# Filler transposes before the first rows of x, and the second sequence's blocks turned in pairs

## The chip, the cores and the metric

The kernel runs on one core of a Trainium2 chip. Four compute engines work side by side, each through its own list of instructions in the order in which the program was built: TensorE (PE; its weight loads are shown apart as PEld), VectorE (DVE), ScalarE (ACT) and GpSimd (POOL). SyncE (SP) computes nothing here and issues DMA transfers. An instruction starts when its engine has reached it and what it waits for is there; one that waits holds up all that stands behind it on its engine. The metric is the device time of one execution in microseconds.

## What is computed

The reference is one encoder layer over two sequences of 512 rows with 1024 features each. It normalizes the rows, projects them, runs a state-space branch (S5, both directions) and an attention branch with a window, merges the two by gates, and ends in a squared-ReLU MLP. For this change only the beginning matters:

```python
def rms_norm(x, g):
    xf = x.astype(jnp.float32)
    y = xf * lax.rsqrt(jnp.mean(xf * xf, axis=-1, keepdims=True) + EPS)
    return (y * g.astype(jnp.float32)).astype(x.dtype)
```

The normalized rows are multiplied with wide weights, among them the 8 blocks of 128 columns that feed the state-space branch ("u"), and 8 blocks each for its two gates. The state-space branch also needs tables: powers of discretized eigenvalues, worked out from a small parameter array (lam) and from coefs.

## The kernel before

**Rows of x.** The 1024 rows are eight tiles of 128 rows (xt; tiles 0 to 3 are the first sequence, 4 to 7 the second), loaded one after the other by SyncE ahead of the weights. square_rows (L287) lets ScalarE square a tile and sum each row (L290), and GpSimd turn the sum into a scale (L292, L293). scale_rows (L295) lets VectorE multiply the tile by it (L296).

**Turning.** turn_rows(s, k) (L298 to L305) takes the k-th block of 128 columns from the four tiles of sequence s, turns each with a transpose on TensorE against the identity (ident, written once at the start by GpSimd) into one PSUM buffer (sps for even k, tps for odd k, two buffers each), and then makes the two halves of a split number: ScalarE writes the high half times the gain (L303), VectorE the remainder, the low half (L304). The traces name these two outputs act.

**Columns.** A column of weights (c_raw, fetched in two halves by SyncE, in fetch, L153) is split the same way: split (L167) lets ScalarE write c_hi (L175) and VectorE c_lo (L176), and after the second half calls for the next c_raw. products (L180) is a generator that issues one matmul at each step, three for each k (high by high, high by low, low by high, 24 in all to a column and sequence), with 128x512 results in one of three PSUM buffers named acc. The generator splits the next column's two halves behind its steps 3 and 9. pull(units) (L260) takes steps from this list, two units a matmul, so pull(6) issues the three matmuls of one k and pull(12) six. some(n) (L388) issues the next n instructions of the tables' arithmetic, small VectorE instructions on 128x64.

**The order of the start.** From L270 on the written order is the order on all five engines. For the first sequence (L399) a loop over k = 0 to 7 turns block k, squares or scales a tile of the second sequence in between, and from k = 2 pulls the three matmuls of an earlier k, so the matmuls stay two blocks behind. Then, for the second sequence:

```python
scale_rows(7)
pull(12)
for k in range(KT):
    turn_rows(1, k)
    pull(6)
    some(4)
```

After this loop come four GpSimd instructions, a small matmul, `while some(4): pull(6)`, and copies of the tables (br_p L429 and L430, ei and er L433 to L435). Behind them the section ends, and from there only TensorE and GpSimd keep the written order; on the others a scheduler places the instructions of tables() (L464 and on) by its own estimates of when they can start, and may lift them into the stretch above. It does so with the load of coefs for the first group (bcx, L469, on SyncE's queue) and with the two copies cw (L480, L481) that read it on VectorE.

Of the kernel before, what the change touches and what calls it, by code (L numbers as in the profile page):

```python
# [19 lines left out]
P = 128  # L20
# [4 lines left out]
KT = D // P  # L25
# [38 lines left out]
def hybrid_layer(ctx, tc, x, rel, onehot, w_qkv, w_ug, vectors, lam, coefs, w_glu, w_out, ln2,  # L64
                 w_up, w_down, out):
    nc = tc.nc
    V, S, PE, GP, SP = nc.vector, nc.scalar, nc.tensor, nc.gpsimd, nc.sync
# [12 lines left out]
    def acc():  # L80
        return ps_acc.tile([P, 512], F32, tag="acc", name="acc")

    def tps():
        return ps_t.tile([P, 512], F32, tag="tps", name="tps")

    def sps():
        return ps_s.tile([P, 512], F32, tag="sps", name="sps")
# [16 lines left out]
    ident = const.tile([P, P], F32, name="ident")  # L104
# [155 lines left out]
    def pull(units):  # L260
        while units > 0:
            cost = next(filler, None)
            if cost is None:
                return
            units -= cost
            phase["units"] -= cost
# [4 lines left out]
    with tc.tile_pool(name="xin", bufs=1, reuse_waits="tile") as xin, tc.tile_pool(name="ssmc", bufs=1) as sc:  # L271
# [23 lines left out]
        def scale_rows(t):  # L295
            V.tensor_scalar_mul(xs[t], xs[t], scales[t])  # L296

        def turn_rows(s, k):  # L298
            ps = tps() if k % 2 else sps()
            for i in range(4):  # L300
                PE.transpose(ps[:, i * P:(i + 1) * P], xs[s * 4 + i][:, k * P:(k + 1) * P], ident)
            h = hT[s][0][:, k, :]
            S.activation(h, ps, AF.Copy, scale=gain_1[:, k:k + 1])  # L303
            V.scalar_tensor_tensor(hT[s][1][:, k, :], ps, gain_1[:, k:k + 1], h.bitcast(F32),  # L304
                                   op0=ALU.mult, op1=ALU.subtract)  # L305
# [82 lines left out]
        def some(n):  # L388
            return len(list(itertools.islice(coefs_left, n)))
# [9 lines left out]
        for k in range(KT):  # L399
            turn_rows(0, k)  # L400
            if k % 2 == 0:
                square_rows(4 + k // 2)
            elif k > 1:
                scale_rows(3 + k // 2)
            if k in (4, 5):
                split(k - 4)
            if k > 1:
                pull(6)
        scale_rows(7)
        pull(12)  # L410
        for k in range(KT):
            turn_rows(1, k)
            pull(6)
            some(4)
        GP.tensor_scalar_mul(gain_q, gain_q, HD ** -0.5)
        GP.tensor_scalar_mul(nsink, nsink, -1.0)
        GP.tensor_tensor(dmask, ident[:, 0:CH], ident[:, 32:32 + CH], op=ALU.add)
# [762 lines left out]
    with tc.tile_pool(name="glu", bufs=1, reuse_waits="tile") as gpool, \  # L1180
# [10 lines left out]
        for u in range(2, 2 * KT):  # L1191
            m, s = divmod(u, 2)
# [436 lines left out]
```

## Time and profile before

| | before |
|---|---|
| median of 3 runs (fastest, slowest) | 1474.6 us (1472.87, 1474.95) |
| profiled execution, its own time | 1474.11 us |
| span of its profile | 1472.3 us |
| TensorE busy, instructions | 1442.3 us (98% of the span), 8074 |
| weight loads busy | 1230.4 us (84%) |
| VectorE busy, instructions | 1101.7 us (75%), 1989 |
| ScalarE busy, instructions | 760.0 us (52%), 1362 |
| GpSimd busy, instructions | 210.4 us (14%), 372 |
| HBM read, written | 173.22 MB, 90.21 MB |

How to read it: the profile comes from one execution. A row of the timeline has the start and the duration in microseconds, the engine, the line, the operation, what it writes and reads with partitions by elements and types, how many instructions of one kind follow each other, and in brackets the idle time of the engine just before and what ended it. Matmuls are pipelined, so their rows overlap and a matmul's row is longer than the distance to the next. A chain row has start, length, engine and line of one piece of the work that ended last, followed back from the end. A row for stretches has the start and end of a stretch, its length, each engine's busy time with its instructions, TensorE's granted clock (1.00 is full), the share of time in which the DMA engines were busy, and what they moved in GB/s. Shares of busy time are means over stages with different limits.

### The profile page before, as it was taken

The page shows a single profiled execution, that of the slowest core. Times are in us where ns is not written, and L with a number is a line of the kernel's source. Part 1 is how long each engine was busy: PE and PEld are TensorE (multiplying, and loading weights), DVE is VectorE, ACT ScalarE, POOL GpSimd, SP SyncE. Part 2 cuts the span into 40 slices and gives each one's busy share as a digit, 9 for nine tenths or more (in the row PEclk, how much of TensorE's full clock was granted, in tenths as well). Part 3 has the DMA queues.
Part 4 walks back from the last instruction along what each step waited for, and adds up shares of the span by engine and source line. Part 5 has one row for each costly group of instructions (what it writes and reads, how often), then busy time and mean ns, then how long its engine had stood idle before and what let it go on. Part 6 is the DMA issues. An engine that isn't in the chain of part 4 may idle for free.

```text
span 1472.3 us, 22141 instructions
## 1 busy us (share of the span) xinstructions
PE 1442.3 (98%) x8074; PEld 1230.4 (84%) x8074; DVE 1101.7 (75%) x1989; ACT 760.0 (52%) x1362; POOL 210.4 (14%) x372
## 2 busy tenths in 40 slices
PE   6999999999999999999999999999999999999998
PEld 4788888879899999998888878888888888888787
DVE  7998859986645899997984588777776597475553
ACT  6677762225535888776343355544544444333332
POOL 3133351002322444222100000000000000000000
PEclk9999999999999999999999999999999999999999
DMA  4455459328940445367553244444443893454441
GB/s 177 142 172 172 165 167 362 116 100 299 346 163 16 144 151 158 107 234 232 191 193 114 86 157 175 148 153 145 146 150 115 326 338 108 158 184 146 127 129 58
DMA packets 102877, 249.16 MB, mean 169 GB/s; under 512 B 12234, under 2 KB 23754, under 8 KB 102768
## 3 DMA queue, kind: packets, MB, share of 16 engines
q1 hardware_dynamic: 60240, 139.55, 29.2%
q0 software_dynamic: 16896, 53.53, 10.5%
q10 hardware_dynamic: 25632, 54.67, 9.9%
q8 instruction: 64, 1.05, 0.3%
q14 instruction: 45, 0.37, 0.1%
HBM read 173.22 MB, written 90.21 MB: 179 GB/s over the span
## 4 chain that ended last, share of the span: by engine, by line
PE 82%; DVE 7%; ACT 4%; DMA 3%; issue 3%; POOL 1%; ACTq 0%; SPq 0%; DVEq 0%; POOLq 0%
PE acc L185 14%; PE bank L117 14%; PE bank L118 13%; PE bank L116 13%; PE acc L813 5%; PE acc L123 3%; PE acc L117 2%; PE acc L118 2%; PE acc L116 2%; PE po L896 2%; PE sps L864 2%; PE sps L547 2%; PE tps L880 2%; PE acc L835 1%; PE sps L645 1%
## 5 line engine op out<-in xcount | busy, mean ns | idle before, releaser
L185 PE MATMUL acc<-act,c_hi 128*128 128x512 f32 x768 | 250.5, 401 | 1.0 <-DVE act L304 0.9
L117 PE MATMUL bank<-b_lo,a_hi 128*128 128x512 f32 x448 | 174.6, 390 | 1.4 <-DVE b_lo L1498 1.4
L118 PE MATMUL bank<-b_hi,a_lo 128*128 128x512 f32 x448 | 174.3, 389 | 0.0
L116 PE MATMUL bank<-b_hi,a_hi 128*128 128x512 f32 x448 | 173.5, 389 | 0.0
L185 PEld LDWEIGHTS acc<-act,c_hi 128*128 128x128 f32 x768 | 142.6, 190 | 29.2 <-DVE act L304 2.4
L185 PE MATMUL acc<-act,c_lo 128*128 128x512 f32 x384 | 153.2, 399 | 0.0
L1497 ACT CAST a_hi<-d_a 128x1024 fp32r<-128x1024 f32 x56 | 59.0, 1054 | 179.3 <-PE bank L117 177.7
L116 PE MATMUL bank<-act,act 128*128 128x512 f32 x368 | 143.3, 389 | 0.5 <-ACT f_sum L1322 0.5
L117 PE MATMUL bank<-act,act 128*128 128x512 f32 x368 | 143.3, 389 | 0.2 <-DVE act L1281 0.2
L118 PE MATMUL bank<-act,act 128*128 128x512 f32 x368 | 143.2, 389 | 0.0
L1498 DVE TENSOR_TENSOR a_lo<-d_a,a_hi 128x1024 fp32r<-128x1024 f32 x56 | 68.5, 1224 | 99.7 <-ACT a_hi L1497 99.7
L813 PE MATMUL acc<-w_hi,act 128*128 128x256 f32 x512 | 114.2, 291 | 0.0
L117 PEld LDWEIGHTS bank<-b_lo,a_hi 128*128 128x128 f32 x448 | 84.1, 188 | 19.6 <-DVE b_lo L1498 2.4
L116 PEld LDWEIGHTS bank<-b_hi,a_hi 128*128 128x128 f32 x448 | 84.1, 188 | 17.6
L118 PEld LDWEIGHTS bank<-b_hi,a_lo 128*128 128x128 f32 x448 | 84.1, 188 | 17.4
L813 PEld LDWEIGHTS acc<-w_hi,act 128*128 128x128 f32 x512 | 87.1, 190 | 3.7
L185 PEld LDWEIGHTS acc<-act,c_lo 128*128 128x128 f32 x384 | 72.8, 190 | 14.0 <-DVE c_lo L176 0.5
L116 PEld LDWEIGHTS bank<-act,act 128*128 128x128 f32 x368 | 69.1, 188 | 15.3 <-ACT f_sum L1322 0.9
L117 PEld LDWEIGHTS bank<-act,act 128*128 128x128 f32 x368 | 69.1, 188 | 14.9 <-DVE act L1281 0.5
L874 ACT ACTIVATE p<-p,nmx 128x257 f32<-128x257 f32 (+1 forms) x128 | 72.1, 564 | 17.9 <-DVE nmx L868 16.7
L118 PEld LDWEIGHTS bank<-act,act 128*128 128x128 f32 x368 | 69.1, 188 | 14.2
L123 PE MATMUL acc<-act,gc_hi 128*128 128x512 f32 x256 | 80.8, 394 | 0.0
(332 smaller groups left out, 3422.1 us busy)
## 6 DMA issues: line engine op xcount, KB each, us to landing
d_a<-a_scr SPq DMA_DIRECT2D x56, 512.0 KB, 3.6
raws<-in_w_up_dram SPq DMA_DIRECT2D x32, 512.0 KB, 4.1
a_scr<-t ACTq DMA_DIRECT2D x64, 256.0 KB, 2.9
k<-in_w_down_dram SPq DMA_DIRECT2D x32, 512.0 KB, 6.1
c_raw<-in_w_ug_dram SPq DMA_DIRECT2D x48, 256.0 KB, 3.7
ct_scr<-ctab POOLq DMA_DIRECT2D x16, 576.0 KB, 3.7
ctab_in<-ct_scr POOLq DMA_DIRECT2D x16, 576.0 KB, 7.4
y_scr<-y_scr POOLq DMA_DIRECT2D x16, 512.0 KB, 5.5
```

Of the source, the lines that this page charges most:

```text
L116: PE.matmul(ps, a[0], b[0], start=first, stop=False)
L117: PE.matmul(ps, a[0], b[1], start=False, stop=False)
L118: PE.matmul(ps, a[1], b[0], start=False, stop=last)
L123: PE.matmul(ps, w[wi][:, k, :], rows[yi], start=k + p == 0, stop=k == KT - 1 and p == 2)
L185: PE.matmul(ps, w[wi][:, k, :], hT[s][hi][:, k, :], start=n == 0, stop=n == 3 * KT - 1)
L547: PE.matmul(ps[:, i * P:(i + 1) * P], bm[:, ri, g, :], u_sb[:, gp * SH + g, :], start=True, stop=True)
L813: PE.matmul(self.ps, hT[sq][act][:, k, col:col + P], w[:, k % 4, :], start=i == 0, stop=i == 3 * KT - 1)
L864: PE.matmul(ps[:, 0:self.nk], qs, kk[:, self.k0 * P:self.k1 * P], start=i == 0, stop=i == 1)
L874: S.activation(p, p, AF.Exp, bias=self.nmx[:, h:h + 1], scale=-1.0, accum_out=self.sums[:, h, self.qb:self.qb + 1])
L880: PE.transpose(pt[:, h * P:(h + 1) * P], self.p[:, h, 1 + i * P:1 + (i + 1) * P], ident)
L1497: S.copy(hi, src)
L1498: V.tensor_sub(lo, src, hi.bitcast(F32))
```

## The change

It has two parts. In turn_rows, the first call (s = 0, k = 0) now issues transposes of the identity into an acc buffer that nothing reads: 32 before the first transpose of x and 8 before each of the three others (busy, L300 to L302 in the changed file). And the loop over the second sequence takes two blocks a turn, with pull(12) and some(8) behind the two, so four transposes and four more stand together, then six matmuls.

```diff
+        idle = acc()
+
+        def busy(n):
+            for i in range(n):
+                PE.transpose(idle[:, i % 4 * P:(i % 4 + 1) * P], ident, ident)
+
         def turn_rows(s, k):
             ps = tps() if k % 2 else sps()
             for i in range(4):
+                if s + k == 0:
+                    busy(8 if i else 32)
                 PE.transpose(ps[:, i * P:(i + 1) * P], xs[s * 4 + i][:, k * P:(k + 1) * P], ident)
...
-        for k in range(KT):
+        for k in range(0, KT, 2):
             turn_rows(1, k)
-            pull(6)
-            some(4)
+            turn_rows(1, k + 1)
+            pull(12)
+            some(8)
```

Lines of the changed file stand 8 or 9 further down: L301, L303 and L304 become L309, L311 and L312, and L429, L469, L480 and L481 become L438, L478, L489 and L490. idle is taken once and takes one of the three acc buffers at the start.

On TensorE the program begins, before, with the blocks of x (xt):

```order
L301 MATMUL sps<-ident,xt 128x128 x4
L301 MATMUL tps<-ident,xt 128x128 x4
L301 MATMUL sps<-ident,xt 128x128 x4
L185 MATMUL acc<-act_103,c_hi 128x512
L185 MATMUL acc<-act_104,c_hi 128x512
```

and after the change with the filler transposes (L302):

```order
L302 MATMUL acc<-ident 128x128 x32
L309 MATMUL sps<-ident,xt 128x128
L302 MATMUL acc<-ident 128x128 x8
L309 MATMUL sps<-ident,xt 128x128
L302 MATMUL acc<-ident 128x128 x8
L309 MATMUL sps<-ident,xt 128x128
L302 MATMUL acc<-ident 128x128 x8
L309 MATMUL sps<-ident,xt 128x128
L309 MATMUL tps<-ident,xt 128x128 x4
```

The four blocks of the first set now stand apart, each behind its filler transposes; from the second set on the order of TensorE is as before until the second sequence's loop.

On VectorE, in the stretch of the first sequence's first blocks, the rows before are these (act_104 is the low half of the first sequence, cw the copies that read bcx):

```order
L176 TENSOR_TENSOR c_lo<-c_raw,c_hi 128x512 x2
L304 SCALAR_TENSOR_TENSOR act_104<-sps,vec,act_103 128x512
L304 SCALAR_TENSOR_TENSOR act_104<-tps,vec,act_103 128x512
L304 SCALAR_TENSOR_TENSOR act_104<-sps,vec,act_103 128x512
L480 TENSOR_TENSOR cw<-bcx 128x128
L481 TENSOR_TENSOR cw<-bcx 128x128
L304 SCALAR_TENSOR_TENSOR act_104<-tps,vec,act_103 128x512
```

and after the change:

```order
L176 TENSOR_TENSOR c_lo<-c_raw,c_hi 128x512 x2
L489 TENSOR_TENSOR cw<-bcx 128x128
L312 SCALAR_TENSOR_TENSOR act_104<-sps,vec,act_103 128x512
L490 TENSOR_TENSOR cw<-bcx 128x128
L312 SCALAR_TENSOR_TENSOR act_104<-tps,vec,act_103 128x512
L312 SCALAR_TENSOR_TENSOR act_104<-sps,vec,act_103 128x512
L312 SCALAR_TENSOR_TENSOR act_104<-tps,vec,act_103 128x512
```

The first copy cw moved ahead of the first low half, the second one behind it; both stood behind the third low half. The diff has no line on this: it is where the scheduler puts them in the changed program.

On ScalarE, behind the second sequence's loop, the rows before are these (c_hi is the high half of a column's weights, up a finished column):

```order
L175 CAST c_hi<-c_raw 128x512
L198 COPY up<-acc 128x8x64
L429 COPY br_p<-pr 64x8x64
L430 COPY br_p<-pr 64x8x64
L207 DMA u_scr<-up 128x1024
L433 COPY ei<-pi 64x512
L434 COPY ei<-pi 64x512
```

and after the change:

```order
L175 CAST c_hi<-c_raw 128x512
L198 COPY up<-acc 128x8x64
L175 CAST c_hi<-c_raw 128x512
L207 DMA u_scr<-up 128x1024
L438 COPY br_p<-pr 64x8x64
L439 COPY br_p<-pr 64x8x64
L442 COPY ei<-pi 64x512
```

The second high half of the next column, which stood behind all copies of ei and er, now stands ahead of br_p, and so does, on VectorE, its low half, behind which the next c_raw is fetched. On SyncE's queue four loads of c_raw now stand between the first load of bcx and the first load of u_sb (a finished column read back), where three stood; the order on GpSimd is as before.

## The prediction

> **What bounds the kernel now.** I read the page's head and chain first, then the chain of the first 62 us in order of time, and then the stretches that the change touches.
>
> ```profile
> span 1472.3 us, 22141 instructions
> PE 82%; DVE 7%; ACT 4%; DMA 3%; issue 3%; POOL 1%; ACTq 0%; SPq 0%; DVEq 0%; POOLq 0%
> ...
> 25.66 1.42 DVE xt L296 x2
> 27.12 0.34 PE sps L301
> ...
> 28.21 0.75 DVE act L304
> ...
> 43.36 0.44 DVE pr L371
> 43.81 0.34 ACT br_p L429
> ...
> 51.37 3.39 DMA c_raw<-in_w_ug_dram
> ```
>
> Over the whole span TensorE is the bound (82% of the chain), but the change lies in the first 60 us, where the chain hops: x must land, TensorE turns its blocks, ScalarE squares the rows of the second sequence, at 25.66 VectorE scales the last of them, TensorE turns them at 27.12, and from 28.21 to 43.8 VectorE's instructions carry it, then ScalarE's and a load of c_raw. Whatever is lost or won ahead of 25.66 is handed on down this list. The next view is busy time by stretch.
>
> ```profile
> core 0: us, PE busy (x) PEld busy (x) DVE busy (x) ACT busy (x) POOL busy (x), PEclk, DMA share, GB/s
> 0.00:12.00 12.00, 1.43 (x3) 0.55 (x3) 5.40 (x21) 7.17 (x12) 6.38 (x18) 1.00 0.86 309
> ...
> 19.00:25.00 6.00, 5.02 (x28) 3.65 (x27) 4.70 (x8) 5.54 (x10) 1.24 (x4) 1.00 0.12 44
> 25.00:44.00 19.00, 18.71 (x94) 14.30 (x95) 17.12 (x56) 8.84 (x16) 2.89 (x7) 1.00 0.05 17
> 44.00:60.00 16.00, 14.91 (x69) 11.63 (x68) 15.31 (x37) 13.06 (x34) 0.31 (x1) 1.00 0.47 148
> 326.20:329.60 3.40, 1.59 (x12) 1.28 (x11) 0.22 (x1) 2.36 (x3) 0.00 (x0) 1.00 0.39 154
> 329.70:333.00 3.30, 3.30 (x13) 2.82 (x12) 0.46 (x1) 2.75 (x5) 0.00 (x0) 0.50 0.00 0
> ```
>
> TensorE stands still for 10.6 of the first 12 us; ScalarE fills 5.54 of the 6.00 us after 19; TensorE idles 0.29 us between 25 and 44 and 1.09 us between 44 and 60. The last two rows show the clock: a stretch with 1.59 of 3.40 us busy is followed by one at a granted 0.50.
>
> **TensorE's clock at the start.** The clock column reads 1.00 before 19 us, but the durations say otherwise.
>
> ```profile
> 7.78 0.48 PE L301 MATMUL sps<-ident,xt 128*128 128x128 f32 x1 [7.78 <-DVE xt L296]
> 9.30 0.48 PE L301 MATMUL sps<-ident,xt 128*128 128x128 f32 x1 [1.05 <-DVE xt L296]
> 11.38 0.48 PE L301 MATMUL sps<-ident,xt 128*128 128x128 f32 x1 [1.60 <-DVE xt L296]
> 12.96 0.47 PE L301 MATMUL sps<-ident,xt 128*128 128x128 f32 x1 [1.10 <-DVE xt L296]
> 13.22 1.06 PE L301 MATMUL tps<-ident,xt 128*128 128x128 f32 x4
> 14.08 1.06 PE L301 MATMUL sps<-ident,xt 128*128 128x128 f32 x4
> 18.14 0.63 PE L185 MATMUL acc<-act,c_lo 128*128 128x512 f32 x1
> ...
> 30.02 0.39 PE L185 MATMUL acc<-act,c_lo 128*128 128x512 f32 x1
> 31.39 0.60 PE L301 MATMUL sps<-ident,xt 128*128 128x128 f32 x4
> ```
>
> The same matmul takes 0.63 us at 18 and 0.39 at 30, four transposes 1.06 and 0.60: the start runs at half clock. Four cold transposes follow each other in 14.08 - 13.22 = 0.86 us, 0.215 each. The first set's four blocks come one by one, as rows of x are scaled: at 7.78, 9.30, 11.38 and 12.96.
>
> **Part one, the filler transposes.** They need ident alone.
>
> ```profile
> 1.03 0.28 POOL masks.py:199 TENSOR_SCALAR_AFFINE_SELECT ident<-ident 128x128 f32<-128x128 f32 x1
> ```
>
> So they start near 1.4 us. 32 x 0.215 = 6.9 us cold, to 8.3; the first rows of x are ready at 7.78. If this busy stretch lifts the clock on the way, as the one from 12.96 to 19 did before, the first group ends before 8, each group of 8 takes about 8 x 0.11 = 0.9 us (half of 0.215 each) inside the 1.5 to 2.1 us between two blocks of x, and the real transposes at 12.96 run in half the time. Then they add nothing, and the whole stretch 13 to 19 could be faster. What that is worth is decided by who is late next, and here the row order of VectorE speaks: the first read of bcx (cw) now stands ahead of the first low half (L304) instead of behind the third.
>
> ```profile
> 8.36 0.33 SPq L469 DMA_DIRECT2D bcx<-in_coefs_dram  x1
> bcx<-in_coefs_dram SPq DMA_DIRECT2D x1, 256.0 KB, 8.4
> ...
> 14.62 0.74 DVE L304 SCALAR_TENSOR_TENSOR act<-sps,vec,act 128x512 fp32r<-128x512 f32 x1
> ...
> 15.41 0.29 PEld L185 LDWEIGHTS acc<-act,c_hi 128*128 128x128 f32 x1 [0.36 <-DVE act L304]
> 15.81 0.75 DVE L304 SCALAR_TENSOR_TENSOR act<-tps,vec,act 128x512 fp32r<-128x512 f32 x1 [0.45 <-ACT act L303]
> 16.47 0.74 DVE L304 SCALAR_TENSOR_TENSOR act<-sps,vec,act 128x512 fp32r<-128x512 f32 x1
> 17.13 0.28 DVE L480 TENSOR_TENSOR cw<-bcx 128x128 f32<-128x128 f32 x1
> 17.33 0.28 DVE L481 TENSOR_TENSOR cw<-bcx 128x128 f32<-128x128 f32 x1
> 17.52 0.69 ACT L303 ACTIVATE act<-tps,vec 128x512 fp32r<-128x512 f32 x1
> ...
> 19.42 0.69 ACT L303 ACTIVATE act<-sps,vec 128x512 fp32r<-128x512 f32 x1 [1.21 <-PE sps L301]
> ```
>
> The bcx transfer is issued at 8.36 and lands 8.4 us later, at 16.76, behind the eight loads of x on the same queue; nothing in the change moves it. Before, cw came at 17.13 and waited for nothing. Now VectorE, which was ready for the first low half at 14.62, stands at cw until 16.78; 0.20 later (17.33 - 17.13) the first low half starts, at 16.98, and ends at 17.73 instead of 15.36: 2.4 us late. Queued behind it are all the other low halves, the scaling of rows 4 to 7 and the next c_lo; and on TensorE the second matmul of the first three waits for it (the 15.41 row), with the transposes of k = 3, 4, 5 behind that, for which ScalarE's L303 waits.
>
> What follows from 17.73, at the two clocks:
> - Full clock: second matmul 0.23, then as from 30.02 (third matmul) to 31.39 + 0.60 = 31.99, the end of the second next four transposes: 1.97. So 17.73 + 0.03 + 2.20 = 19.96, and L303 of k = 4 starts at 19.98 against 19.42: **+0.56 us**. (The second low half, 16.98 + 0.66 + 0.20 = 17.84 to 18.59, is in time.)
> - Half clock throughout: before, the same chain took 19.42 - (14.62 + 0.74) = 4.06 us. 17.73 + 4.06 = 21.79: **+2.4 us**.
>
> From L303 of k = 4 on ScalarE is nearly full, so this shift reaches 27.1 and, over VectorE's full stretch, everything behind it. Which clock? TensorE has nothing to do from about 14.3 (12.96, plus 0.24 for the warm last block, 8 x 0.11 for two more sets and 0.23 for one matmul) to 17.76, some 3.4 us. A shorter gap cost the clock later on:
>
> ```profile
> 328.93 0.71 PE L645 MATMUL sps<-st,ctab_in 128*128 128x128 f32 x4 [1.81 <-ACT st L615]
> ```
>
> After this 1.81 us gap the clock was at 0.50 for 3.3 us. I expect the same in or just behind the new gap, for part of the chain, and take the middle: **+1.5 us**, bounds +0.56 and +2.4. [...]
>
> **Part two, blocks in pairs.** Instruction counts stay: 32 transposes, 48 matmuls, 8 of L303 and L304, 32 of some(). On TensorE four transposes go ahead of three matmuls, and the columns in this loop read the first sequence, so they wait for none of it. TensorE idles only 0.29 us from 25 to 44, so at most 0.3 can be gained; VectorE is the bound and its list is only permuted, 0.66 us a low half with L303 coming at a similar pace: 0, bounds -0.3 and +0.3.
>
> The new order reaches one stage further: the second half of the next c_hi and c_lo goes ahead of the br_p copies.
>
> ```profile
> 49.06 0.62 ACT L175 CAST c_hi<-c_raw 128x512 fp32r<-128x512 f32 x1
> ...
> 50.66 0.69 DVE L176 TENSOR_TENSOR c_lo<-c_raw,c_hi 128x512 fp32r<-128x512 f32 x1
> ...
> 54.78 0.62 ACT L175 CAST c_hi<-c_raw 128x512 fp32r<-128x512 f32 x1 [1.82 <-DMA c_raw<-in_w_ug_dram]
> ...
> 56.79 0.87 PE L534 MATMUL tps<-ident,bpre 128*128 128x128 f32 x6 [0.34 <-DVE bpre L511]
> ```
>
> The c_hi of 49.06 moves ahead of the br_p copy of 43.81, its c_lo with it, so the c_raw load of 51.37 is issued some 6 us sooner and ScalarE's 1.82 us wait can go; SP's u_sb load goes behind one more c_raw, by 0.33 us of issue. TensorE can win at most the 1.09 us it idles from 44 to 60. Against that, 0.62 us of ScalarE and 0.69 of VectorE are put in front of the chain to the first transposes of the tables, for which TensorE waits at 56.79 (VectorE's bpre): up to 0.6 us lost. The two sides overlap; I take 0, bounds -1.1 and +0.6.
>
> **Sum.** The profiled execution took 1474.11 us, 1.8 more than its span and 0.5 under the median of 1474.6. 1474.11 + 1.5 + 0 + 0 = **1475.6 us**.
>
> **Rivals.**
> 1. *The clock gain comes through.* If bcx is in by 14.7, or VectorE's wait is covered, the transposes of k = 4 end before 18 at full clock, and ScalarE's 1.21 us of waiting before L303 of k = 4 goes, and some 0.2 more with an earlier k = 3 (17.52 row): k = 4 starts near 18.0, -1.4 us, 1472.7; with the whole of the -1.1 it is 1471.6. For: everything but bcx is there. Against: DMA is busy 0.86 of the first 12 us, and the landing would have to be 2 us sooner.
> 2. *The clock stays at half until after 24 us* (slower). If transposes do not lift it, the filler takes 6.9 us, each group of 8 another 1.7, and the first set ends at 8.3 + 3 x 1.72 + 4 x 0.215 + 0.25 = 14.6 instead of 12.96 + 0.47 = 13.43; bcx still hides that, but TensorE is cold at 17.76: +2.4. A cold k takes 3 x 0.43 + 0.86 = 2.15 us; ScalarE asks for k = 6 about 1.1 us after k = 5, so a clock not full by 24 us adds 1.05: +3.5, 1477.6. It decides from a wake-up later than 24. For: the busy stretch from 12.96, which began with transposes, was lifted only at 19. Against: the stretch from 329.7 was lifted within 3.3 us, so from 17.76 the clock should be back at about 21 to 23. [...] The trace cannot settle it: no stretch of transposes alone stands in it.
> 3. *The shift is given back* in the 1.09 us of idle between 44 and 60: within 0.5 of before, 1474.1.
>
> **Chances.** Forecast 0.60; rival 1, 0.14; rival 2, 0.15; rival 3, 0.11. A difference under 0.2% (2.95 us) is about what a measurement can tell from none. Half of the first rival (with the whole of part two's gain and a lucky run: the shown runs span 2.1 us) reaches past -0.2%, and most of the second, with a few of the forecast's upper end, past +0.2%: faster 0.07, same 0.79, slower 0.14. Range: from rival 1 with part two's gain, 1471.6, to rival 2 with part two's loss, 1477.6 + 0.6 = 1478.2, each end a fourth of the run spread further out: 1471.1 to 1478.7.
>
> **What would show it.** VectorE's cw starting at about 16.8 behind an idle of some 2 us laid to the bcx load, the first L304 ending near 17.7; TensorE idle near 14.3 to 17.8; L303 of k = 4 near 20 (full clock) or 21 to 22 (half); filler transposes of 0.11 us spacing at some point before 8 if they lift the clock, 0.215 to the end if not; c_raw issued near 45. I am wrong if cw does not wait, if the first low half ends before 16, or if the stages from 60 on stand more than 3 us from where they stood.

## The result

| | before | changed kernel |
|---|---|---|
| median of 12 runs | 1474.41 us | 1477.16 us |
| ratio to before, 95% interval | 1 | 1.0023, 1.0014 to 1.0032 |
| profiled execution, its own time | 1474.11 us | 1475.65 us |
| span of its profile | 1472.3 us | 1473.9 us |
| TensorE busy, instructions | 1442.3 us, 8074 | 1448.0 us, 8130 |
| VectorE busy | 1101.7 us | 1101.3 us |

The changed kernel is slower by 0.23%; between the two profiled executions it is 1.54 us, and the forecast was +1.5 us. One of the 12 runs of the changed kernel, 2421 us long at a mean granted clock of 0.556, is left out of the ratio, and the median of its other 11 runs is 1476.62 us, 2.21 above before.

First the chain that ended last, in order of time, of the changed kernel: start, length, engine and line of each piece.

```profile
1.64 6.51 DMA xt<-in_x_dram
8.17 8.39 DMA bcx<-in_coefs_dram
16.79 0.76 DVE act L312
17.59 0.75 PE acc L185 x2
18.34 0.85 PE tps L309 x4
...
27.60 1.42 DVE xt L296 x2
29.07 0.34 PE sps L309
...
46.16 0.43 DVE pr L379
46.62 1.19 ACT br_p L438
```

The load of bcx is now on the chain: it follows the load of x and ends at 16.56, and the first low half (L312) follows it. The scaling of the last two tiles (L296) starts at 27.60, where it was 25.66 before: **1.94 us late**. br_p comes at 46.62 instead of 43.81, 2.81 late.

Next VectorE's timeline around the first low half, and under it TensorE's and ScalarE's in the same stretch.

```profile
13.25 1.29 DVE L176 TENSOR_TENSOR c_lo<-c_raw,c_hi 128x512 fp32r<-128x512 f32 x2
16.58 0.29 DVE L489 TENSOR_TENSOR cw<-bcx 128x128 f32<-128x128 f32 x1 [2.04 <-DMA bcx<-in_coefs_dram]
16.79 0.74 DVE L312 SCALAR_TENSOR_TENSOR act<-sps,vec,act 128x512 fp32r<-128x512 f32 x1
```

```profile
1.36 5.24 PE L302 MATMUL acc<-ident 128*128 128x128 f32 x32 [1.36 <-POOL ident masks.py:199]
...
7.95 1.04 PE L302 MATMUL acc<-ident 128*128 128x128 f32 x8
...
13.91 0.49 PE L185 MATMUL acc<-act,c_hi 128*128 128x512 f32 x1
17.59 0.50 PE L185 MATMUL acc<-act,c_hi 128*128 128x512 f32 x1 [3.19 <-DVE act L312]
17.93 0.41 PE L185 MATMUL acc<-act,c_lo 128*128 128x512 f32 x1
18.16 1.03 PE L309 MATMUL tps<-ident,xt 128*128 128x128 f32 x4
...
21.36 0.69 ACT L311 ACTIVATE act<-sps,vec 128x512 fp32r<-128x512 f32 x1 [1.45 <-PE sps L309]
```

VectorE, free at 14.54, stands 2.04 us at cw for bcx. Behind it TensorE stands 3.19 us at its second matmul. The filler transposes did lift the clock (eight of them take 1.04 us from 7.95 on), and one matmul right behind the gap still takes 0.41 us (17.93); but from 18.16 four transposes take 1.03 us again, as at half clock. The stretches say the same in the column of the granted clock, the third from the end (busy times engine after engine, then PEclk, DMA share, GB/s). First the changed kernel:

```profile
12.00:19.00 7.00, 3.44 (x21) 2.61 (x20) 4.89 (x11) 3.91 (x7) 1.69 (x4) 0.94 0.83 308
19.00:25.00 6.00, 6.00 (x30) 4.85 (x29) 3.59 (x7) 4.33 (x8) 0.79 (x2) 0.78 0.01 3
```

and the first of the two stretches in the kernel before:

```profile
12.00:19.00 7.00, 6.04 (x22) 4.99 (x23) 5.70 (x13) 4.60 (x8) 1.70 (x5) 1.00 0.86 324
```

TensorE is busy for 3.44 of the 7 us from 12 to 19, where it was 6.04 before the change, and its clock is 0.78 in the next 6 us. ScalarE's high half of k = 4 starts at 21.36 instead of 19.42, and with it the 1.94 us are there.

Last, ScalarE and SyncE's queue behind the second sequence's loop:

```profile
45.49 0.62 ACT L175 CAST c_hi<-c_raw 128x512 fp32r<-128x512 f32 x1
46.62 1.19 ACT L438 COPY br_p<-pr 64x512 f32<-64x512 f32 x1 [0.51 <-DVE pr L379]
...
52.85 0.62 ACT L175 CAST c_hi<-c_raw 128x512 fp32r<-128x512 f32 x1
...
46.28 1.71 SPq L165 DMA_DIRECT2D c_raw<-in_w_ug_dram  x2
...
62.28 1.06 ACT L561 COPY h<-sps 64x504 f32<-64x504 f32 x1 [1.65 <-PE sps L556]
```

The kernel before has this row for the first copy of h:

```profile
60.95 1.07 ACT L552 COPY h<-sps 64x504 f32<-64x504 f32 x1 [0.76 <-PE sps L547]
```

The load of c_raw that was issued at 51.37 before is the second of the two in the row of 46.28; that row ends at 47.99, so it goes out some 4 us sooner. (Counted from the second load of bcx on, four loads of c_raw now stand ahead of the first of u_sb, and three before.) The c_hi at 52.85 no longer waits, where it waited 1.82 us before. The first copy of h starts at 62.28 instead of 60.95: of the 2.81 us at br_p 1.33 are left, **1.5 us won back**.

### The profile page after: what moved, and what is told of

The parts are those of the page before. It is cut to its first block, busy times and chain, and to the rows that moved or that the text cites. A ratio compares the mean times of both kernels' runs of the same rounds, so it can differ in the third digit from the quotient of the medians.

```text
span 1473.9 us, 22251 instructions
## 1 busy us (share of the span) xinstructions
PE 1448.0 (98%) x8130; PEld 1237.2 (84%) x8130; DVE 1101.3 (75%) x1989; ACT 759.4 (52%) x1362; POOL 210.6 (14%) x372
## 4 chain that ended last, share of the span: by engine, by line
PE 83%; DVE 6%; issue 4%; ACT 3%; DMA 2%; POOL 1%; ACTq 0%; SPq 0%; DVEq 0%; POOLq 0%
PE acc L185 14%; PE bank L117 14%; PE bank L118 13%; PE bank L116 13%; PE acc L822 5%; PE acc L123 3%; PE po L905 2%; PE acc L117 2%; PE acc L118 2%; PE acc L116 2%; PE sps L873 2%; PE tps L889 2%; PE sps L556 2%; PE acc L844 1%; DMA toep<-toep_scr 1%
```

## The experiments

**Theory.** One row decides: the first cw stands ahead of the first low half, waits for bcx, and TensorE idles long enough to lose its clock. **Rivals:** the pairs cost the time; the filler transposes cost it in themselves; the stall alone costs it, whatever the clock does.

Three places of the profile are followed in all runs: the scaling of the last two tiles (L296 before), br_p (L429) and the first copy of h (L552). Times in us; "clock up" is the first record of the full clock, "half" the stretches at half clock after it, without the one that most profiles have at their very end.

| run | scaling | br_p | h | clock up | half | ratio to before, 95% |
|---|---|---|---|---|---|---|
| before | 25.66 | 43.81 | 60.95 | 19.0 | 329.6 to 333.0 | 1 |
| the change | 27.60 | 46.62 | 62.28 | 4.5 | 18.2 to 21.6, 393.6 to 397.1 | 1.0023 (1.0014, 1.0032) |
| change_again | 27.95 | 46.97 | 62.64 | 5.2 | 15.5 to 22.3, 332.9 to 336.3, 865.4 to 868.8 | one run, 1478.9 us |
| fill_only | 28.02 | 46.18 | 63.35 | 6.0 | 16.3 to 23.1, 862.8 to 866.2 | 1.0025 (1.0016, 1.0034) |
| pairs_only | 24.34 | 43.34 | 58.98 | 16.4 | none | 0.9998 (0.9989, 1.0007) |
| pairs_again | 25.62 | 44.63 | 60.27 | 18.8 | 329.4 to 332.8 | 0.9997 (0.9989, 1.0006) |
| keep_warm | 26.06 | 45.06 | 60.70 | 4.1 | none | 1.0009 (1.0000, 1.0018) |
| cw_on_gpsimd | 23.91 | 42.93 | 59.09 | 6.6 | none | 1.0005 (0.9996, 1.0014) |
| cw_late | 23.89 | 42.91 | 58.56 | 5.1 | none | 0.9994 (0.9985, 1.0002) |
| cw_late_again | 23.42 | 42.44 | 58.08 | 4.1 | 328.4 to 331.8 | 1.0000 (0.9991, 1.0009) |
| fill_cw_late | 23.42 | 41.59 | 58.42 | 5.8 | 859.1 to 862.6 | 1.0002 (0.9993, 1.0011) |
| fill_16 | 23.49 | 42.52 | 58.19 | 4.4 | 7.8 to 11.2, 857.7 to 861.1 | 1.0000 (0.9991, 1.0009) |

### One part alone: fill_only and pairs_only

fill_only is the changed kernel with the old loop:

```diff
-        for k in range(0, KT, 2):
+        for k in range(KT):
             turn_rows(1, k)
-            turn_rows(1, k + 1)
-            pull(12)
-            some(8)
+            pull(6)
+            some(4)
```

> Only the filler transposes; the second sequence's loop as before. Theory (VectorE stands at cw for bcx, TensorE idles and its clock falls, ScalarE comes late): cw at 16.6 behind 2 us of waiting, the scaling of the last two tiles of x at 27.6 as in the changed kernel (25.66 before), br_p at 43.81 + 1.94 = 45.75, the wait of ScalarE for c_raw (1.82 us before) still there, and the whole +1.9 us (ratio 1.0013). Rival (the loss belongs to the pairs): the scaling at 25.66 +- 0.3, the whole within 0.3 us of before.

The whole loss is in this part: 1.0025, about twice the 1.0013 expected. cw waits 2.01 us, and the lateness is larger than the 1.94 expected (28.02 - 25.66 = 2.36), since here the half clock lasted twice as long. It goes on unchanged over br_p (+2.37) and h (+2.40), and the wait for c_raw is still there:

```profile
17.54 0.79 PE L185 MATMUL acc<-act,c_hi 128*128 128x512 f32 x1 [3.14 <-DVE act L312]
18.13 0.63 PE L185 MATMUL acc<-act,c_lo 128*128 128x512 f32 x1
...
57.15 0.62 ACT L175 CAST c_hi<-c_raw 128x512 fp32r<-128x512 f32 x1 [1.84 <-DMA c_raw<-in_w_ug_dram]
```

At 18.13 the matmul takes 0.63 us, the half-clock length; in the changed kernel's profile it took 0.41 at the same place.

pairs_only is the kernel before with the loop of the change and nothing else:

```diff
-        for k in range(KT):
+        for k in range(0, KT, 2):
             turn_rows(1, k)
-            pull(6)
-            some(4)
+            turn_rows(1, k + 1)
+            pull(12)
+            some(8)
```

> Only the pairs; no filler transposes. Theory: nothing changes up to 25.66; br_p some 0.86 us late (44.7), since the changed kernel went from +1.94 to +2.80 between these two places; c_raw issued some 5 us sooner and ScalarE's wait of 1.82 gone, which gives back 1.4; the tables' copies at 60 us 0.6 sooner than before, the whole -0.6 us (ratio 0.9996). Rival (the loss belongs to the pairs): the whole +1.5 us or more.

0.9998, so the pairs make no loss. The scaling at 24.34 was not expected: the code up to there is that of before, and yet it is 1.32 us sooner. The clock of this execution rose at 16.4 us instead of 19.0, and the matmuls show it:

```profile
15.83 0.63 PE L185 MATMUL acc<-act,c_lo 128*128 128x512 f32 x1
16.26 0.65 PE L301 MATMUL tps<-ident,xt 128*128 128x128 f32 x4
...
17.22 0.39 PE L185 MATMUL acc<-act,c_lo 128*128 128x512 f32 x1
```

The moment at which the clock rises thus differs between executions of the same instructions, and two single profiles can differ by 1.3 us at 26 us for that reason alone. So the pairs are judged from one place to the next: from the scaling to br_p 19.00 us against 18.15 before (0.85 lost), from br_p to h 15.64 against 17.14 (1.50 won), 0.65 won in all; the second run says the same (19.01 and 15.64).

### The stalled row moved: cw_on_gpsimd, cw_late and fill_16

cw_on_gpsimd gives the first group's two cw to another engine; the arithmetic is the same:

```diff
                 for src, dst in ((bb[:, 0:2], bb[:, 2:4]), (cx, cw)):
-                    V.tensor_add(dst[:, 0], src[:, 0], src[:, 1])
-                    V.tensor_sub(dst[:, 1], src[:, 0], src[:, 1])
+                    by = GP if c == 0 and dst is cw else V
+                    by.tensor_tensor(dst[:, 0], src[:, 0], src[:, 1], op=ALU.add)
+                    by.tensor_tensor(dst[:, 1], src[:, 0], src[:, 1], op=ALU.subtract)
```

> The whole change, but the first group's two cw are computed by GpSimd, so VectorE has nothing that waits for bcx. Theory: the first low half at 14.5 instead of 16.8, no half clock after 4.4 us, ScalarE's high half of k = 4 near 18.0 (21.36 in the changed kernel, 19.42 before), the scaling of the last tiles at 24.2 (27.60; 25.66), br_p 0.5 us sooner than before, the whole 1.9 us under before (ratio 0.9987). Rival (the fillers themselves or something else behind them cost the time): the scaling still at 27 or later and the whole 1 us or more over before. Second rival (ScalarE or VectorE are late there for other reasons): the scaling within 0.3 us of 25.66.

Up to br_p as expected (23.91, and 0.88 sooner than before at br_p), and the loss is gone: 1.0005, its interval below that of fill_only. The gain of 1.9 us in the whole did not come. A part of it went to what this edit brings with it, between br_p and h, 16.16 us here against 15.64 in both profiles of the pairs. The first two rows are of cw_on_gpsimd, the other two of pairs_only:

```profile
48.86 1.02 DVE L447 TENSOR_TENSOR es<-er,ei 128x576 f32<-128x576 f32 x1
49.80 0.55 DVE L486 TENSOR_TENSOR bb<-bb,tw 128x128 f32<-128x128 f32 x1
...
49.29 0.75 DVE L439 TENSOR_TENSOR es<-er,ei 128x576 f32<-128x576 f32 x1
49.95 0.28 DVE L478 TENSOR_TENSOR bb<-bb,tw 128x128 f32<-128x128 f32 x1
```

GpSimd computed its cw at 48.6 to 50.2, and these two VectorE instructions took 1.02 and 0.55 us beside it, where in the profile of pairs_only they took 0.75 and 0.28: 0.54 together. So the row was moved in another way. cw_late keeps cw on VectorE, with a column of ones that is written where cw should stand:

```diff
             turn_rows(0, k)
+            if k == 2:
+                V.memset(one, 1.0)
...
+                    for i, op in enumerate((ALU.add, ALU.subtract)):
+                        if c == 0 and dst is cw:
+                            V.scalar_tensor_tensor(dst[:, i], src[:, 0], one, src[:, 1], op0=ALU.mult, op1=op)
```

> The whole change; the first group's two cw stay on VectorE but read a column of ones that VectorE writes behind the third low half, so they stand where they stood before the change. Theory (the order of these two on VectorE is the whole loss): the first low half at 14.5, the scaling of the last two tiles of x near 23.9 (27.60 in the changed kernel, 25.66 before), br_p 0.9 us before the time of before, the tables' copies at 60 us 1.9 to 2.4 sooner than in the profile of before, and the whole 1 to 2 us under before (ratio 0.9986 to 0.9993). Rival (in cw_on_gpsimd nothing was won although VectorE did not wait: the gain of the early clock is taken back behind 60 us, or the clock is lost again in other executions): the same profile up to 60, but the ratio 1.000 or above, and a mean granted clock of 0.999 or less in half of the executions. Second rival (GpSimd's own cw cost it there, VectorE's es and bb ran 0.27 us longer each beside them): ratio 0.9990 or less, with the clock as in the rival.

```profile
14.52 0.74 DVE L313 SCALAR_TENSOR_TENSOR act<-sps,vec,act 128x512 fp32r<-128x512 f32 x1
...
16.93 0.06 DVE L411 MEMSET vec<- 128x1 f32 x1
17.04 0.62 DVE L494 SCALAR_TENSOR_TENSOR cw<-bcx,vec 128x128 f32<-128x128 f32 x2
```

The first low half stands at 14.52 again and cw waits for nothing at 17.04. With everything else of the change in place the ratio is 0.9994 (0.9985, 1.0002): the interval lies wholly below that of the change (1.0014 to 1.0032). This is the test that settles the cause, since nothing else moved: in the traces the two kernels have the same instructions in the same order on TensorE, ScalarE, GpSimd and SyncE, and on VectorE all but the two cw and the column of ones are in the same order. The same holds for fill_only and fill_cw_late, at 1.0025 and 1.0002. So one place in one engine's list makes the difference, 0.0029 here and 0.0023 by the repeat of cw_late (1.0000), 3.4 to 4.3 us.

fill_16 reaches the same without touching cw: 16 filler transposes at the start instead of 32, and the scheduler puts cw where it was.

```diff
-                    busy(8 if i else 32)
+                    busy(8 if i else 16)
```

> The whole change with 16 filler transposes at the start instead of 32; the scheduler then puts the two cw behind the third low half, as before. Theory (the place of cw makes the loss, not the fillers): VectorE does not wait at cw, the scaling of the last tiles between 24.0 and 25.7 according to when the clock rises, the whole as with the pairs alone, ratio 0.9990 to 1.0003. Rival (fillers cost time in themselves): ratio 1.001 or more.

```profile
16.49 0.28 DVE L489 TENSOR_TENSOR cw<-bcx 128x128 f32<-128x128 f32 x1
```

1.0000, and no wait at cw, which stands behind the third low half. The scaling at 23.49 was sooner than the 24.0 to 25.7 expected, because the clock, lost at 7.8 after TensorE had idled 2.86 us behind the first 16, came back at 11.2 under the groups of 8, before the real work began. No loss from the fillers as such is seen in the ratio.

### The stall with the clock held: keep_warm

```diff
+            if k == 2:
+                pull(2)
+                busy(24)
+                pull(4)
-            if k > 1:
+            elif k > 1:
                 pull(6)
```

24 more transposes of the identity stand behind the first matmul, in the gap; VectorE's wait stays.

> The whole change, and 24 more filler transposes behind the first matmul, in the gap in which TensorE waits for VectorE. VectorE still stands at cw until 16.6. Theory (the stall costs 0.56 us at full clock and the lost clock the rest of the 1.94): granted clock full through 13 to 25 us, the high half of k = 4 at 19.9, the scaling of the last tiles at 26.2, the whole within 0.3 us of before (+0.56 - 0.58; ratio 1.000). Rival (the lost clock costs nothing, ScalarE and VectorE are late by the stall alone): the scaling at 27.6 and the whole +1.5 us as in the changed kernel.

```profile
14.10 2.78 PE L302 MATMUL acc<-ident 128*128 128x128 f32 x24
17.48 0.50 PE L185 MATMUL acc<-act,c_hi 128*128 128x512 f32 x1 [0.60 <-DVE act L312]
...
18.04 0.60 PE L309 MATMUL tps<-ident,xt 128*128 128x128 f32 x4
...
12.00:19.00 7.00, 6.03 (x46) 5.12 (x45) 4.78 (x11) 4.25 (x8) 1.73 (x4) 1.00 0.85 315
19.00:25.00 6.00, 5.39 (x31) 3.94 (x29) 4.99 (x8) 5.55 (x11) 0.93 (x3) 1.00 0.13 45
```

The second matmul starts at 17.48, as late as in the change (17.59), but the four transposes behind it take 0.60 us instead of 1.03, the granted clock stays at 1.00, and the scaling comes at 26.06 instead of 27.60: 1.54 us of the 1.94 were the lost clock, and the stall at full clock leaves 0.40 against before (25.66 to 26.06, the prediction had 0.56). But before begins at half clock. Against cw_late, the same fillers without the stall (23.89), the stall alone cost 2.17 us (2.64 against cw_late_again) and the lost clock 1.54 more, 3.71 in all: the larger part is the wait, which the gain of the early clock had hidden. The ratio, 1.0009 where 1.000 was expected, lies between the change and cw_late, but its interval (1.0000, 1.0018) touches both of theirs.

### Repeats: change_again, cw_late_again, pairs_again and fill_cw_late

> The changed kernel once more, for a second profile. Theory: cw again at 16.6 +- 0.3 behind 2 us of waiting for bcx, and a half-clock stretch that begins within 14.5 to 18.5; it lasts one or two times 3.41 us, so the scaling of the last tiles comes between 26.3 and 28.1. Rival (the half clock after the stall was chance): full clock from 5 to 25 us in this execution and the scaling at 26.3 or sooner.

The stall and the loss of the clock came again: cw at 16.46 behind 2.09 us of waiting, half clock from 15.5 to 22.3, the scaling at 27.95 (+2.29). So it is no chance of one execution. In all eleven runs of the change that the ratio uses the mean granted clock is 0.996 to 0.998; of 33 runs of before that were taken beside the first four experiments, 28 have 1.000.

The last three kernels ask whether the fillers are worth anything once nothing waits; fill_cw_late is cw_late with the old loop.

> cw_late a second time, beside the pairs alone and the fillers alone in the same comparison, to see what the filler transposes are worth once VectorE does not wait. Theory (they are worth the clock that starts 9 to 14 us sooner than in before, which rises at 16.4 in one profile and 19.0 in another): 1 us under pairs_again, ratio to before 0.9985 to 0.9998. Rival (worth nothing: half-clock stretches later in the execution take it back): within 0.0005 of pairs_again in the ratio.

> The pairs alone a second time. Theory: the pairs gain 0.7 us between 26 and 60 us (0.84 lost up to br_p, 1.53 won back by the sooner c_raw), and nothing after that: ratio 0.9990 to 1.0000. Rival (the 0.7 us is taken back later): 1.0000 to 1.0006.

> The filler transposes with the two cw kept behind the third low half, and the second sequence's loop as before. Theory: the scaling of the last tiles near 23.9, the tables' copies at 60 us 1.7 sooner than in the profile of before (no 0.7 of the pairs), ScalarE's wait of 1.82 for c_raw still there; ratio 0.9988 to 1.0000 and some 0.0005 above cw_late_again. Rival (fillers worth nothing in the whole): ratio 1.0000 to 1.0008.

Up to h they win something: h comes at 58.56 and 58.08 in the two profiles of cw_late, against 58.98 and 60.27 in those of the pairs alone, and with the old loop at 58.42 against 60.95 in before. In the whole this is not seen: the ratios of cw_late (narrowly), cw_late_again and fill_cw_late lie above those expected, and the last two are as their rivals had it. 1.0000, 0.9997 and 1.0002 cannot be told apart, and neither can cw_late's 0.9994: the fillers' 0.4 to 2.5 us at 60 us are not in the total.

Where they go is settled in part. A sign named with the rival to cw_late came true: its mean granted clock was below 1.000 in 6 of 11 runs, in cw_late_again and fill_cw_late in 7 of 11 each, and in 9 of the 48 runs of before beside them. So these kernels lose the clock more often than before; at which places in each run is not on record. One place where it happens shows near 860 us, where TensorE waits for rows that VectorE normalizes (rn_xn) behind a load of the MLP's weights (raws). The first row is of before, the other two of fill_cw_late:

```profile
860.32 1.06 PE L1287 MATMUL sps<-ident,rn_xn 128*128 128x128 f32 x8 [0.49 <-DVE rn_xn L1273]
...
858.37 1.23 PE L1301 MATMUL sps<-ident,rn_xn 128*128 128x128 f32 x8 [1.93 <-DVE rn_xn L1287]
...
859.20:862.50 3.30, 3.30 (x11) 2.62 (x10) 3.30 (x7) 2.81 (x5) 0.00 (x0) 0.50 0.00 0
```

On the chain the load takes 4.75 to 4.87 us in before, in both profiles of the pairs and in keep_warm, and TensorE stops for 0.49 to 0.61. In the change, cw_on_gpsimd, cw_late and cw_late_again it takes 5.23 to 5.63, with stops of 0.97 to 1.38; in change_again, fill_only, fill_cw_late and fill_16 6.21 to 6.40, with stops of 1.93 to 2.13, and in these four the clock falls for 3.4 us. Why the load is longer is not shown, and each of these is one execution. Another place was seen in the profile of cw_late_again, where the DMA engines are full:

```profile
345.00:360.00 15.00, 14.17 (x97) 12.66 (x96) 9.57 (x16) 9.08 (x18) 5.00 (x7) 1.00 1.02 353
...
375.00:390.00 15.00, 13.71 (x111) 12.96 (x110) 8.39 (x16) 7.17 (x15) 4.45 (x7) 1.00 1.02 367
...
359.18 0.46 PE L657 MATMUL sps<-u_sb,toep 128*128 128x128 f32 x2 [0.83 <-DMA toep<-toep_scr]
...
380.18 0.46 PE L657 MATMUL sps<-u_sb,toep 128*128 128x128 f32 x2 [0.87 <-DMA toep<-toep_scr]
```

The DMA share is 1.02, and TensorE, which filled 15.00 us of both stretches in the profile of before, idles 0.83 and 1.29 us in them, partly at waits for toep. But the share is 1.00 in before too, and cw_late, with the same code and a share of 1.01, kept its lead over this stretch, so this is a place where executions differ, not an explanation of the average.

## Why the prediction held, step by step

- **cw waits for bcx: right.** Forecast 16.78 behind some 2 us, measured 16.58 behind 2.04; the first low half ended at 17.53, forecast 17.73. cw_late and fill_16 show by their ratios that this place in VectorE's list is the whole loss, as far as intervals of 0.0009 to each side can tell.
- **The fillers lift the clock and hide: right.** The first 32 took 5.24 us, less than the 6.9 of 32 cold ones, and were over at 6.6, ahead of x at 7.8; the real transposes from 12.97 on took 0.60 a set. The ratios of fill_16 and cw_late show no loss from them. Rival 2, in the form that transposes do not lift the clock, is excluded: nothing but transposes ran on TensorE up to 4.5 us, when the full clock began.
- **The clock is lost in the gap: right, its size set too low.** TensorE idled 3.19 us (forecast 3.4), and the half clock came right behind. The term was the middle, +1.5, of 0.56 and 2.4; the profiles measured +1.94, +2.29 and +2.36 at the scaling. The half clock did not cover a part of the chain but lasted 3.4 us, or 6.8 in the other two, and nearly the whole chain to L303 of k = 4 lies inside. The bounds held; the upper one was the better value. The row that it was argued from, the stop of 1.81 us with half clock behind it, is weaker than it looked: the same stop stands in all twelve profiles, between 326 and 332 us, and the clock fell behind it in four of them.
- **The pairs: the sum within its bounds, two parts missed.** Taken as 0 in the loop and 0 behind it; measured 0.85 lost up to br_p and 1.50 won behind it, 0.65 won. Of the 0.85, about 0.6 is the c_lo that moved ahead of br_p, which the prediction had named as a loss but counted behind the loop, and 0.23 a wait of VectorE for ScalarE at the second pair's first low half. The 1.5 is the wait for c_raw, which went as described. It is more than the 1.1 that the prediction allowed there from TensorE's idle time; but four of TensorE's instructions moved ahead of br_p (73 between br_p and h in pairs_only, 77 before), so the two parts can only be judged together.
- **Rivals 1 and 3.** Rival 1, bcx in time, did not occur; cw_late is what it would have looked like, and its -1.4 us at L303 of k = 4 was -1.76 there (17.66), without a gain in the whole that can be told from none. Rival 3, the shift given back up to 60 us, did not occur: 1.33 were left.
- **The whole: +0.23% where +0.10% was forecast.** The sum was made against profiled executions, and these differ by 1.54 us, as forecast. That it fits so closely is luck in part. The term of 1.5 was 1.94 and the pairs' 0 was a gain, which left 1.33 at h; and behind that place each of the two executions lost the clock for one more stretch of 3.4 us, at 329.6 and at 393.6. Most runs of before have no such stretch: their mean clock of 1.000 leaves no room for it (0.5 x 3.4 of 1470 us is 0.0012). So the medians differ by more, 2.21 us (1476.62 against 1474.41). What else spreads the change's runs from 1474.56 to 1480.63 us was not tried.

## What to carry to other kernels

Look at the built order of every engine, not only at the lines that a change touches: filler work on one engine shifted a scheduler's estimates and put an instruction that waits for a transfer ahead of the critical list of another. If a free instruction may be placed early, tie it to a point behind which it cannot stall (one small dependency did it here). And where an idle gap as long as this one (3.1 to 3.2 us, three profiles of three) comes ahead of a chain on TensorE, price the chain at half clock, not at a mean.

## What the runs showed of the hardware

- The moments at which the clock rose or fell were not fixed to the program: the same code got the full clock at 16.4 and at 18.8 us (pairs_only, pairs_again), and the half-clock stretches lasted 3.4 us (18.2 to 21.6 in the change) or 6.8 (16.3 to 23.1 in fill_only). With the two moments the scaling of the last tiles came at 24.34 and at 25.62, 1.3 us apart between executions of one kernel.
- Float32 transposes of the identity alone lifted the clock: with them it was full after 4.1 to 6.6 us in all kernels that begin with 32, and 24 of them held it through a wait (keep_warm, 1.00 from 12 to 25 us).
- After the stop of 3.19 us and after stops of 3.14 and 3.23 (fill_only, change_again) the clock was lost each time, in two of the three already within the stop. Stops of up to 1.2 us between the groups of fillers (1.19 ahead of 7.79 in the change), and the 0.84 us in cw_on_gpsimd's profile at 15.3, did not cost it. In between the executions differ: behind the stop of 1.81 us near 330 the clock fell in four profiles of twelve.
- What decides between the two is not shown. In before that stop ended at 328.93, and the granted clock was 0.50 from 329.7 to 333.0; in the change it ended at 330.17, and the granted clock was 1.00 from 328.80 to 335.60. No run was made to test it.
